# A conditioned decoder trunk in 3-pass fp32r: the first weight slab in plain fp32, first inputs split on two engines, a TensorE run-in, a sixth raw buffer

## The chip, the cores and the metric

The kernel runs on one core of a Trainium2 chip. The metric is the device time of one execution in microseconds (us). Six engines' rows appear in the profile: PE (TensorE matmul), PEld (TensorE weight load), DVE (VectorE), ACT (ScalarE), POOL (GpSimd) and SP (SyncE, which issues the DMAs here).

## The reference

The reference is a decoder trunk of two layers, width 1024, 256 tokens, batch 1. Every sub-layer gets a shift, a scale and a gate from a conditioning vector:

```python
def swiglu(u, w_in, w_out):
    gate, up = jnp.split(u @ w_in, 2, axis=-1)
    return (jax.nn.silu(gate) * up) @ w_out
...
c_act = jax.nn.silu(c)
for l in range(DEPTH):
    mod = c_act @ mod_w[l] + mod_b[l]
    sh1, sc1, g1, ... = jnp.split(mod, 9, axis=-1)
    f = swiglu(x * (1 + sc1) + sh1, ffn_in[l, 0], ffn_out[l, 0])
    x = layer_norm(ALPHA * x + 0.5 * (1 + g1) * f, ...)
    ...   # a mixer (RG-LRU and GLA in layer 0, latent attention in layer 1), then a second swiglu
```

What matters here is the start: the very first matmul needs x * (1 + sc1) + sh1, and sc1 and sh1 need a product of the silu of c with 2 x 1024 x 1024 modulation weights.

## The kernel before, in words

Everything is kept transposed: features on the 128 partitions, the 256 tokens along the free axis. A weight matrix is cut into 128 x 128 tiles, and the host writes the tiles in the exact order of use into `wst`, as slabs of 16 tiles (1 MB). `Stream` (L300) reads this one long list. A slab is loaded into a raw buffer (pool `wraw`, five buffers of 1 MB, L238), and each half of it (8 tiles) is converted by `conv_to` (L329): ScalarE writes the rounded half `whi` (L338), VectorE writes the remainder `wlo` (L339). Three fp32r matmuls then make one product of near-fp32 precision (`mm3`, L403): high weight by high input (L407), high weight by low input (L408), low weight by high input (L409). The inputs are split in the same way by `split` (L443 to L445) into `uhi` and `ulo`.

The modulation weights `modw` use the same raw buffers, in slabs of 1 MB with two 128 x 1024 blocks each. VectorE multiplies a block with the silu of c and sums along the row (`junk`, L388): one block gives one column of a modulation vector. The first eight modulation slabs hold, for each block k of the model width, the shift and the scale of block k.

The first swiglu runs in passes over its 22 pairs of output tiles. The first pass takes 8 pairs (16 PSUM halves) over k = 0 to 3, the second takes 8 other pairs over k = 0 to 7, the third goes back to the first 8 pairs for k = 4 to 7. One k of a pass uses exactly one slab: 16 tiles, 48 matmuls of 256 columns. Step k of the first pass needs, in this order: modulation slab k, the block k of x (`xT`), weight slab k. They are issued in that order on the queue of SP, which runs in order; an issue whose raw buffer is still in use holds all issues behind it. `first_u` (L497) makes input block k: the two `junk` sums, 1 + scale (`scp`, L507, VectorE), the modulated input (`ut`, L509, ScalarE), `uhi` (L444, ScalarE), `ulo` (L445, VectorE) and the scaled residual (`ax`, L511, ScalarE).

The order of instructions on each engine is not written out. A planner sets it at build time, from the order of the program (earlier has priority) and its own idea of when an operand will be there. On the chip each engine then keeps that order, waiting where an operand is late.

Of the kernel before, what the change touches and what calls it, by code (L numbers as in the profile page):

```python
# [11 lines left out]
F32 = mybir.dt.float32  # L12
# [7 lines left out]
MULT, ADD, SUB, MAX, MIN = ALU.mult, ALU.add, ALU.subtract, ALU.max, ALU.min  # L20

P = 128
DM = 1024
KD = DM // P
SEQ = 256
DEPTH = 2
DFF = 2816
NJ = DFF // P
# [22 lines left out]
GLATE = 30  # L51
PAUSE = False
EOFF = 60

FROW = 320
PADS = (128, 64, 416, 352)
# [175 lines left out]
def trunk_kernel(ctx: ExitStack, tc: tile.TileContext, xT, cvec, pos, wst, modw, colsd,  # L232
                 rgw, wa2, outT):
    nc = tc.nc
    sync, act, vec, pool, pe = nc.sync, nc.scalar, nc.vector, nc.gpsimd, nc.tensor

    const = ctx.enter_context(tc.tile_pool(name="const", bufs=1))
    wraw = ctx.enter_context(tc.tile_pool(name="wraw", bufs=5))  # L238
    whi = ctx.enter_context(tc.tile_pool(name="whi", bufs=4))


# [11 lines left out]
    def nm(s):  # L253
        uid[0] += 1
        return f"{s}_{uid[0]}"

    def T(pl, shape, dt=F32, tag=None, **kw):
        return pl.tile(shape, dt, tag=tag, name=nm(tag), **kw)
# [9 lines left out]
    def mmps():  # L268
        return T(ps_mm, [P, 512], tag="mm")
# [19 lines left out]
    ones_dm = constant(1.0 / DM, [P, P], "ones_dm")  # L289
# [6 lines left out]
    ident = T(const, [P, P], tag="ident")  # L296
# [3 lines left out]
    class Stream:  # L300
# [28 lines left out]
        def conv_to(self, n):  # L329

            self.dma_to((n - 1) // 2 + Stream.RAW)
            W2 = Stream.HS * P
            while self.nconv < min(n, 2 * NSLAB):
                s = self.nconv
                hi = T(whi, [P, W2], F32R, tag="whi")
                lo = T(wlo, [P, W2], F32R, tag="wlo")
                raw = self.raw[s // 2][:, (s % 2) * W2:(s % 2 + 1) * W2]
                act.activation(hi, raw, AF.Copy)  # L338
                i = vec.tensor_tensor(lo, raw, hi.bitcast(F32), SUB)  # L339
                if self.behind is not None:  # L340
                    queue_behind(i, self.behind)
                self.conv[s] = (hi, lo)
                if s % 2:
                    self.raw.pop(s // 2)
                self.nconv += 1
                if self.todo and not self.pause and self.todo[0][2] <= s // 2:
                    self.reduce()
                    if len(self.todo) > 4 and self.todo[0][2] <= s // 2:
                        self.reduce()

        def next(self, *keys):
            n = len(keys)
            assert tuple(PLAN[self.pos:self.pos + n]) == keys, (PLAN[self.pos], keys)
            s, o = divmod(self.pos, Stream.HS)
            assert o + n <= Stream.HS
            if o == 0:
                self.conv_to(s + 1 + Stream.AHEAD)
                self.conv.pop(s - 1, None)
            self.pos += n
            hi, lo = self.conv[s]  # L360
            sl = slice(o * P, (o + n) * P)
            return hi[:, sl], lo[:, sl]


        def mod_target(self, s):
# [34 lines left out]
    x0 = T(main, [P, KD, SEQ], tag="yy")  # L400
    W = Stream()

    def mm3(ps, wt, mv, start, stop, shared=False):  # L403

        hi, lo = wt
        mh, ml = mv
        pe.matmul(ps, hi, mh, start=start, stop=False, skip_group_check=shared)  # L407
        pe.matmul(ps, hi, ml, start=False, stop=False, skip_group_check=shared)  # L408
        pe.matmul(ps, lo, mh, start=False, stop=stop, skip_group_check=shared)  # L409

    def queue_behind(i, j):
        tc.add_manual_dep(i.ins, j.ins.name, mybir.DependencyInfo(
            mybir.DependencyClass.NoSync, mybir.DependencyReason.DATA), reason="order")
# [24 lines left out]
    for i in range(2):  # L438
        ps = mmps()
        pe.matmul(ps, one_row, crow[:, i * 512:(i + 1) * 512], start=True, stop=True)  # L440
        ta(cact[:, i * 512:(i + 1) * 512], ps, AF.Silu)

    def split(src, hi, lo):  # L443
        act.activation(hi, src, AF.Copy)  # L444
        vec.tensor_tensor(lo, src, hi.bitcast(F32), SUB)  # L445


    uhi = T(main, [P, KD, SEQ], F32R, tag="uhi")
    ulo = T(main, [P, KD, SEQ], F32R, tag="ulo")
# [6 lines left out]
    def u(k):  # L456
        return uhi[:, k, :], ulo[:, k, :]
# [35 lines left out]
    scp0 = T(const, [P, KD], tag="scp0")  # L493
# [3 lines left out]
    def first_u(k):  # L497
        if k in first_done:
            return
        first_done.add(k)  # L500

        W.mods_to(k + 1)
        while W.todo and W.todo[0][0] < 2 * k + 2:
            W.reduce()
        kk = slice(k, k + 1)
        sc0, sh0 = W.modcols[(0, SC)], W.modcols[(0, SH)]
        vec.tensor_scalar(scp0[:, kk], sc0[:, kk], 1.0, None, ADD)  # L507
        ut = T(wk, [P, SEQ], tag="ut")
        act.activation(ut, x0[:, k, :], AF.Identity, bias=sh0[:, kk], scale=scp0[:, kk])  # L509
        split(ut, uhi[:, k, :], ulo[:, k, :])  # L510
        act.mul(ax[:, k, :], x0[:, k, :], ALPHA)  # L511


    class Boundary:
# [79 lines left out]
        def stats(self, y, ysq):  # L594
# [38 lines left out]
            for m, f in early(*self.next):  # L633
                ps = mmps()
                for k in range(KD):
                    mm3(ps[:, :SEQ + 2], W.next((m, k, f)), [t[:, k, :SEQ + 2] for t in self.ya], k == 0, k == KD - 1)
                with tc.high_priority(offset=EOFF):
                    wab = T(wk, [P, 2], tag="wab", bufs=4)
# [52 lines left out]
    def ffn(l, i, prev):  # L691
        with tc.tile_pool(name=nm("ffn"), bufs=1) as fp:
            hhi = T(fp, [P, NJ, SEQ], F32R, tag="hhi")
            hlo = T(fp, [P, NJ, SEQ], F32R, tag="hlo")
            m = ("ffn_in", l, i)

            def glu(j, pg, pu, bg=0.0, bu=0.0, off=100):
                with tc.high_priority(offset=off):
                    sg = T(wk, [P, SEQ], tag="sg")
                    ta(sg, pg, AF.Silu, bias=bg)  # L700
                    h = T(wk, [P, SEQ], tag="h")
                    vec.scalar_tensor_tensor(h, pu, bu, sg, ADD, MULT)  # L702
                    split(h, hhi[:, j, :], hlo[:, j, :])

            for j in range(EARLY if prev else 0):
                (pg, bg), (pu, bu) = prev.values[2 * j:2 * j + 2]
                glu(j, pg, pu, bg, bu)

            passes = ffn_passes(l, i)
            part = {}  # L710
            for g, ks in passes:
                grp = {j: mmps() if q < 6 else axps() for q, j in enumerate(g)}
                for k in ks:
                    prev.u(k) if prev else first_u(k)
                    for j in g:
                        for half in range(2):
                            mm3(grp[j][:, half * SEQ:(half + 1) * SEQ], W.next((m, k, half * NJ + j)), u(k),
                                k == ks[0] and half == 0, k == ks[-1], True)
                if ks[-1] < KD - 1:
                    keep = [flat(q) for q in range(2)]  # L720
                for q, j in enumerate(g):
                    ps = grp[j]
                    if ks[-1] < KD - 1:
                        part[j] = keep[q // 4][:, (q % 4) * 512:(q % 4 + 1) * 512]
                        act.activation(part[j], ps, AF.Copy)
                        continue
                    off = GOFF
                    if j in part:
                        off -= GLATE * q
                        with tc.high_priority(offset=off):  # L730
                            vec.tensor_tensor(part[j], ps, part[j], ADD)  # L731
                        ps = part[j]
                    glu(j, ps[:, :SEQ], ps[:, SEQ:], off=off)
            if prev:
                prev.residual()
            for j in range(max(g.stop for g, _ in passes), NJ):
                pp = [mmps(), mmps()]
                for half in range(2):
                    for k in range(KD):
                        mm3(pp[half][:, :SEQ], W.next((m, k, half * NJ + j)), u(k),  # L740
                            k == 0, k == KD - 1)
                glu(j, pp[0][:, :SEQ], pp[1][:, :SEQ])
            if l == 0 and i == 0:
                rg_decay()
            if l == 1 and i == 0:
                rope_tables()
            bd = Boundary(l, 0 if i == 0 else 2, 0.5)
            for f in range(KD):
                ps = mmps()
                for k in range(NJ):  # L750
                    mm3(ps[:, :SEQ], W.next((("ffn_out", l, i), k, f)), (hhi[:, k, :], hlo[:, k, :]),
                        k == 0, k == NJ - 1)
                    if f == 1 and k == NJ // 2:
                        bd.shift_out()
                bd.tile_out(f, ps[:, :SEQ])
        return bd
# [559 lines left out]
```

## Time and profile before

| what | us |
|---|---|
| median of 3 runs | 1040.61 |
| lowest and highest of them | 1035.38, 1040.7 |
| the profiled execution, its own time | 1033.83 |
| span of the profiled execution (first to last instruction) | 1032.1 |
| TensorE busy in that span | 995.5 |
| VectorE busy in that span | 884.7 |
| first matmul on a weight slab starts at | 12.03 |

All rows below are from the profiled execution. Its own time lies 1.7 us above its span and 6.8 us below the median of the runs. A row of a timeline gives the start, the busy time, the engine, the line, what is written from what, and in brackets how long the engine had been idle and what released it. TensorE's rows overlap, since matmuls are pipelined: the distance of two starts is the time that one matmul costs.

### The profile page before, as it was taken

The numbers are of one execution on the slowest core, as the hardware profiler recorded it, in microseconds if no ns is written. First come the engines' busy times: TensorE is split into PE (matmuls) and PEld (weight loads), VectorE is DVE, ScalarE is ACT, GpSimd is POOL, SyncE is SP. The second block draws the span as 40 slices with busy tenths as digits, with TensorE's granted clock in tenths as the row PEclk, the third lists the DMA queues.
The fourth block names the chain that finished last, engine by engine and source line by source line (L and its number), as shares of the span: only waits on it lengthen the run. The fifth ranks groups of instructions, "written<-read, shape, count | busy, mean of one in ns | idle before, by whom it ended". The sixth has DMA issues, their size and how long they took to land.

```text
span 1032.1 us, 20703 instructions
## 1 busy us (share of the span) xinstructions
PE 995.5 (96%) x8338; PEld 972.8 (94%) x8338; DVE 884.7 (86%) x1491; ACT 612.5 (59%) x1023; POOL 54.8 (5%) x72
## 2 busy tenths in 40 slices
PE   6999999999999989999999999999999999999995
PEld 5999999998899979999999999999998889999995
DVE  5789999797998989999998899998888799666664
ACT  4746654567886656745545665455559666545543
POOL 0000010000001020000030000002000200000200
PEclk9999999999999999999999999999999999999998
DMA  9998798554466943699977469898743146665621
GB/s 342 366 339 319 257 368 309 208 204 169 170 264 242 350 185 142 245 361 373 365 279 286 166 251 371 322 359 321 286 167 129 73 164 245 246 224 187 243 83 41
DMA packets 38578, 258.57 MB, mean 251 GB/s; under 512 B 4289, under 2 KB 6849, under 8 KB 7762
## 3 DMA queue, kind: packets, MB, share of 16 engines
q1 hardware_dynamic: 38482, 257.25, 66.7%
q8 instruction: 65, 1.06, 0.4%
q14 instruction: 31, 0.25, 0.1%
HBM read 256.18 MB, written 1.05 MB: 249 GB/s over the span
## 4 chain that ended last, share of the span: by engine, by line
PE 82%; DVE 11%; issue 2%; ACT 2%; DMA 2%; POOL 0%; SPq 0%; DVEq 0%; ACTq 0%
PE mm L409 25%; PE mm L407 25%; PE mm L408 25%; DVE wlo L339 4%; DVE junk L388 2%; DMA wraw<-modw 1%; ACT whi L338 1%; DVE flat L557 1%; DVE yy L581 1%; PE ax L408 1%; PE ax L407 1%; PE ax L409 1%; DVE acc L589 1%; DVE flat L731 0%; DMA rgt<-rgw 0%
## 5 line engine op out<-in xcount | busy, mean ns | idle before, releaser
L339 DVE TENSOR_TENSOR wlo<-wraw,whi 128x1024 fp32r<-128x1024 f32 x340 | 416.7, 1233 | 81.3 <-ACT whi L338 80.8
L338 ACT ACTIVATE whi<-wraw 128x1024 fp32r<-128x1024 f32 x340 | 357.6, 1058 | 212.4 <-PE mm L408 138.0
L407 PE MATMUL mm<-uhi,whi 128*128 128x256 f32 x1672 | 461.4, 278 | 11.5 <-ACT uhi L444 6.0
L409 PE MATMUL mm<-uhi,wlo 128*128 128x256 f32 x1672 | 460.1, 277 | 3.6 <-DVE wlo L339 3.6
L408 PE MATMUL mm<-ulo,whi 128*128 128x256 f32 x1672 | 462.1, 277 | 0.7 <-DVE ulo L445 0.6
L407 PEld LDWEIGHTS mm<-uhi,whi 128*128 128x128 f32 x1672 | 313.6, 188 | 14.9 <-ACT uhi L444 7.9
L409 PEld LDWEIGHTS mm<-uhi,wlo 128*128 128x128 f32 x1672 | 313.8, 188 | 4.2 <-DVE wlo L339 4.1
L408 PEld LDWEIGHTS mm<-ulo,whi 128*128 128x128 f32 x1672 | 314.8, 188 | 1.5 <-DVE ulo L445 1.2
L409 PE MATMUL mm<-hhi,wlo 128*128 128x256 f32 x704 | 194.6, 276 | 1.9 <-DVE wlo L339 1.9
L408 PE MATMUL mm<-hlo,whi 128*128 128x256 f32 x704 | 194.4, 276 | 0.0
L407 PE MATMUL mm<-hhi,whi 128*128 128x256 f32 x704 | 194.3, 276 | 0.0
L388 DVE CUSTOM_DVE_ANT_0 junk<-wraw,cact,cols 128x1024 bf16<-128x1024 f32 x144 | 184.9, 1284 | 5.7 <-DMA wraw<-modw 5.0
L409 PEld LDWEIGHTS mm<-hhi,wlo 128*128 128x128 f32 x704 | 132.1, 188 | 2.3 <-DVE wlo L339 2.3
L407 PEld LDWEIGHTS mm<-hhi,whi 128*128 128x128 f32 x704 | 132.2, 188 | 0.0
L408 PEld LDWEIGHTS mm<-hlo,whi 128*128 128x128 f32 x704 | 132.2, 188 | 0.0
L571 POOL TENSOR_TENSOR ax<-ax,shift 128x256 f32<-128x256 f32 x42 | 42.2, 1039 | 734.7 <-ACT shift L569 734.7
L444 ACT ACTIVATE hhi<-h 128x256 fp32r<-128x256 f32 x88 | 35.9, 413 | 44.3 <-DVE h L702 43.2
L585 ACT ACTIVATE ysq<-yy 128x256 f32<-128x256 f32 x42 | 17.4, 414 | 51.8 <-DVE yy L581 50.0
L702 DVE SCALAR_TENSOR_TENSOR h<-mm,sg 128x256 f32<-128x256 f32 x75 | 30.9, 418 | 7.9 <-PE mm L409 7.9
L581 DVE SCALAR_TENSOR_TENSOR yy<-mm,gate,ax 128x256 f32<-128x256 f32 x48 | 22.8, 478 | 16.2 <-PE mm L409 15.0
L445 DVE TENSOR_TENSOR hlo<-h,hhi 128x256 fp32r<-128x256 f32 x88 | 36.0, 417 | 0.0
L429 ACT ACTIVATE sg<-mm 128x256 f32<-128x256 f32 x75 | 27.4, 366 | 3.0 <-DVE h L702 1.7
(288 smaller groups left out, 1088.1 us busy)
## 6 DMA issues: line engine op xcount, KB each, us to landing
wraw<-wst SPq DMA_DIRECT2D x169, 1024.0 KB, 5.8
wraw<-modw SPq DMA_DIRECT2D x71, 1024.0 KB, 6.5
wraw<-modw SPq DMA_DIRECT2D x2, 512.0 KB, 5.4
yy<-xT SPq DMA_DIRECT2D x8, 128.0 KB, 6.8
wraw<-wst SPq DMA_DIRECT2D x2, 512.0 KB, 7.9
rgt<-rgw SPq DMA_DIRECT2D x8, 128.0 KB, 3.7
outT<-yy SPq DMA_DIRECT2D x3, 256.0 KB, 2.6
outT<-yy SPq DMA_DIRECT2D x2, 128.0 KB, 2.6
```

Source lines behind the costliest of these rows:

```text
L338: act.activation(hi, raw, AF.Copy)
L339: i = vec.tensor_tensor(lo, raw, hi.bitcast(F32), SUB)
L388: i = vec.tensor_tensor_reduce(junk, t, cact, 1.0, col("mod_b", (l * NMOD + v) * KD + j), MULT, ADD, self.modcols[(l, v)][:, j:j + 1])
L407: pe.matmul(ps, hi, mh, start=start, stop=False, skip_group_check=shared)
L408: pe.matmul(ps, hi, ml, start=False, stop=False, skip_group_check=shared)
L409: pe.matmul(ps, lo, mh, start=False, stop=stop, skip_group_check=shared)
L429: i = act.activation(out, in_, func, **kw)
L444: act.activation(hi, src, AF.Copy)
L445: vec.tensor_tensor(lo, src, hi.bitcast(F32), SUB)
L571: pool.tensor_tensor(ax[:, j, :], ax[:, j, :], shift, SUB)
L581: vec.scalar_tensor_tensor(y, ps, self.gate[:, f:f + 1], ax[:, f, :], MULT, ADD)
L702: vec.scalar_tensor_tensor(h, pu, bu, sg, ADD, MULT)
```

## The change

Four edits. The first slab (`RAWSLABS = 1`, so k = 0 of the first pass) is not converted: its 16 tiles are multiplied as plain fp32, one matmul each in place of three, with the unsplit `ut` as the input. That input is split after this use (ScalarE and VectorE, L444 and L445), for the second pass. For k from 1 on, `uhi` is computed by VectorE directly from x, while ScalarE computes `ut`; the ScalarE pass `uhi` is gone for these seven blocks. In the program's order, the conversion of the first half of slab 1 and the whole of `first_u(1)` now stand ahead of the matmuls of k = 0. Twelve plain fp32 matmuls of an identity with a constant (128 columns each) are placed behind the two small matmuls that spread c over the partitions; their result is not used. The pool of raw buffers has six buffers.

```diff
-    wraw = ctx.enter_context(tc.tile_pool(name="wraw", bufs=5))
+    wraw = ctx.enter_context(tc.tile_pool(name="wraw", bufs=6))
...
+                if s < 2 * RAWSLABS:
+                    self.conv[s] = (self.raw[s // 2][:, (s % 2) * W2:(s % 2 + 1) * W2], None)
+                    if s % 2:
+                        self.raw.pop(s // 2)
+                    self.nconv += 1
+                    continue
...
+        if lo is None:
+            pe.matmul(ps, hi, mv, start=start, stop=stop, skip_group_check=shared)
+            return
...
+    ps = mmps()
+    for i in range(NWARM):
+        pe.matmul(ps[:, :P], ident, ones_dm, start=True, stop=True)
...
-        split(ut, uhi[:, k, :], ulo[:, k, :])
+        if k < RAWSLABS:
+            u_raw[k] = ut
+        else:
+            vec.tensor_scalar(uhi[:, k, :], x0[:, k, :], scp0[:, kk], sh0[:, kk], MULT, ADD)
+            u_last[0] = vec.tensor_tensor(ulo[:, k, :], ut, uhi[:, k, :].bitcast(F32), SUB)
+            first_ax(k)
...
+                    if not prev and k < RAWSLABS and part == {}:
+                        W.conv_to(2 * RAWSLABS + 1)
+                        first_u(k + 1)
...
+                    if not prev and k in u_raw:
+                        queue_behind(split(u_raw.pop(k), uhi[:, k, :], ulo[:, k, :]), u_last[0])
+                        first_ax(k)
```

## Rows read from the trace of the kernel before

**Rows 1.** The page, busy time, share of the span and instructions by engine.

```profile
PE 995.5 (96%) x8338; PEld 972.8 (94%) x8338; DVE 884.7 (86%) x1491; ACT 612.5 (59%) x1023; POOL 54.8 (5%) x72
```

**Rows 2.** Windows: length, busy us (count) by engine, clock, DMA share, GB/s.

```profile
0.00:12.03 12.03, 3.75 (x4) 1.16 (x4) 3.65 (x13) 5.27 (x10) 1.41 (x14) 1.00 0.78 253
12.03:20.01 7.98, 7.91 (x49) 7.62 (x49) 6.25 (x10) 4.05 (x6) 0.00 (x0) 1.00 1.03 423
20.01:26.46 6.45, 5.60 (x50) 5.40 (x48) 4.74 (x9) 2.54 (x6) 0.00 (x0) 1.00 1.01 414
26.46:33.61 7.15, 5.76 (x49) 5.57 (x49) 5.44 (x9) 3.23 (x6) 0.00 (x0) 1.00 1.01 418
33.61:39.05 5.44, 5.44 (x47) 5.44 (x48) 4.82 (x5) 5.44 (x8) 0.00 (x0) 1.00 0.93 361
```

**Rows 3.** The chain that ended last, 0 to 45 us: start, us, what.

```profile
14.41 1.28 DVE junk L388
15.74 1.28 DVE junk L388
17.07 0.16 DVE scp L507
17.26 0.61 ACT ut L509
17.89 0.42 ACT uhi L444
18.31 0.96 ACT whi L338
19.30 2.36 DVE wlo L339 x2
...
33.61 0.38 PE mm L407
```

**Rows 4.** ACT's timeline, 14 to 62 us.

```profile
14.74 0.42 ACT L511 ACTIVATE ax<-yy 128x256 f32<-128x256 f32 x1 [1.80 <-DMA yy<-xT]
...
18.22 2.00 ACT L338 ACTIVATE whi<-wraw 128x1024 fp32r<-128x1024 f32 x2
...
60.90 0.60 ACT L509 ACTIVATE ut<-yy,mod,scp 128x256 f32<-128x256 f32 x1 [3.62 <-DVE scp L507]
61.41 2.00 ACT L338 ACTIVATE whi<-wraw 128x1024 fp32r<-128x1024 f32 x2
```

**Rows 5.** PE's timeline, 12 to 34 us.

```profile
12.03 1.23 PE L407 MATMUL mm<-uhi,whi 128*128 128x256 f32 x4 [5.96 <-ACT uhi L444]
...
16.05 0.41 PE L407 MATMUL mm<-uhi,whi 128*128 128x256 f32 x1
16.26 0.41 PE L408 MATMUL mm<-ulo,whi 128*128 128x256 f32 x1
...
26.46 0.39 PE L407 MATMUL mm<-uhi,whi 128*128 128x256 f32 x1 [0.85 <-ACT whi L338]
...
33.61 0.38 PE L407 MATMUL mm<-uhi,whi 128*128 128x256 f32 x1 [1.39 <-ACT whi L338]
```

**Rows 6.** PE's timeline at 293 us: plain fp32 matmuls of 256 columns, two rows each.

```profile
293.18 0.59 PE L836 MATMUL ax<-ya,rgt 128*128 128x256 f32 x2
293.61 0.59 PE L835 MATMUL ax<-ya,rgt 128*128 128x256 f32 x2
```

**Rows 7.** Groups by line and shape on DVE: names, shapes, count | busy us, mean ns.

```profile
L673 DVE TENSOR_SCALAR yy<-xh,cols 128x256 f32<-128x256 f32 x2 | 0.8, 413 | 0.1
```

**Rows 8.** PE's timeline, 273 to 279 us.

```profile
273.93 0.38 PE L409 MATMUL mm<-uhi,wlo 128*128 128x256 f32 x1 [1.02 <-DVE wlo L339]
...
278.45 0.38 PE L409 MATMUL mm<-uhi,wlo 128*128 128x256 f32 x1 [1.50 <-DVE wlo L339]
```

**Rows 9.** DVE's timeline at 258 us.

```profile
257.99 1.28 DVE L388 CUSTOM_DVE_ANT_0 junk<-wraw,cact,cols 128x1024 bf16<-128x1024 f32 x1 [0.32 <-DMA wraw<-modw]
```

**Rows 10.** The chain that ended last, 235 to 282 us.

```profile
261.28 4.88 DMA rgt<-rgw
```

More of the change, by code (lines that the diff above doesn't have):

```diff
@@ L53 @@
 EOFF = 60
+RAWSLABS = 1
+NWARM = 12
 FROW = 320
@@ L361, in next @@
             sl = slice(o * P, (o + n) * P)
-            return hi[:, sl], lo[:, sl]
+            return hi[:, sl], None if lo is None else lo[:, sl]
         def mod_target(self, s):
@@ L441, in trunk_kernel @@
         ta(cact[:, i * 512:(i + 1) * 512], ps, AF.Silu)
+    ps = mmps()
+    for i in range(NWARM):
+        pe.matmul(ps[:, :P], ident, ones_dm, start=True, stop=True)
     def split(src, hi, lo):
         act.activation(hi, src, AF.Copy)
-        vec.tensor_tensor(lo, src, hi.bitcast(F32), SUB)
+        return vec.tensor_tensor(lo, src, hi.bitcast(F32), SUB)
     uhi = T(main, [P, KD, SEQ], F32R, tag="uhi")
@@ L509, in first_u, with first_ax @@
         act.activation(ut, x0[:, k, :], AF.Identity, bias=sh0[:, kk], scale=scp0[:, kk])
-        split(ut, uhi[:, k, :], ulo[:, k, :])
+        if k < RAWSLABS:
[4 more added lines that the diff above has]
+            first_ax(k)
+    u_raw = {}
+    u_last = [None]
+    def first_ax(k):
         act.mul(ax[:, k, :], x0[:, k, :], ALPHA)
@@ L714, in ffn @@
                     prev.u(k) if prev else first_u(k)
+                    if not prev and k < RAWSLABS and part == {}:
+                        W.conv_to(2 * RAWSLABS + 1)
+                        first_u(k + 1)
                     for j in g:
                         for half in range(2):
-                            mm3(grp[j][:, half * SEQ:(half + 1) * SEQ], W.next((m, k, half * NJ + j)), u(k),
+                            wt = W.next((m, k, half * NJ + j))
+                            mm3(grp[j][:, half * SEQ:(half + 1) * SEQ], wt, u_raw[k] if wt[1] is None else u(k),
                                 k == ks[0] and half == 0, k == ks[-1], True)
+                    if not prev and k in u_raw:
+                        queue_behind(split(u_raw.pop(k), uhi[:, k, :], ulo[:, k, :]), u_last[0])
+                        first_ax(k)
                 if ks[-1] < KD - 1:
```

## The prediction

> **What bounds the kernel now.** I read the page first, then the windows cut at the starts of the steps k, then the chain of the first 45 us, then the timelines of ScalarE and TensorE inside it. The page makes it a TensorE kernel: 995.5 of 1032.1 us busy [rows 1]. All four edits lie in the first 34 us, where this does not hold. TensorE has no weight to multiply until 12.03 [rows 5], its steps k = 0, 1 and 2 take 7.98, 6.45 and 7.15 us, and only k = 3 runs at its own pace: 48 matmuls in 5.44 us, 0.113 each [rows 2]. Up to 33.61 the chain holds no step that TensorE sets [rows 3]. What repeats in it is a ring between VectorE and ScalarE, once for each k: two sums `junk` (1.28 each, 2.66 from start to start of the next thing), `scp`, `ut`, `uhi`, the first conversion `whi`, two conversions `wlo`, and the sums of the next k. One turn is 7.15 us, the length of the window of k = 2 [rows 2]. TensorE is served by it and waits 0.85 us before k = 2 and 1.39 us before k = 3 [rows 5]. From 33.61 on TensorE sets the end. So the question for each edit is whether it moves the start of k = 3. What moves that start, moves the end by as much, as long as nothing later takes it back.
>
> DMA is the ring's other partner: it is busy without a break from 12 to 34 us at 414 to 423 GB/s [rows 2]. Block 1 of x landed at 14.74 [rows 4]. Modulation slab 1 was issued just ahead of it, so by estimate it landed 0.13 MB / 423 GB/s = 0.31 us earlier, at 14.43, and weight slab 1, issued just behind, lands 1.05 MB / 423 GB/s = 2.48 us later, at 17.2. By the same estimate weight slab 2 lands at 22.5 and slab 3 at 27.8, each with its modulation slab and block of x ahead of it.
>
> **The change, part by part.**
>
> *First slab in plain fp32.* It removes two conversions on ScalarE and two on VectorE (`wlo`, 2.36 for two [rows 3]) and the split of block 0 ahead of the first matmul. So the first matmul can start when `ut` is there. Its place in the ring is `scp` + `ut`, and whether k = 0 is early or late, the sums of k = 1 start when their modulation slab is there: 14.43 by the estimate, against 14.41 in the trace, where they came right behind the second `wlo` [rows 3]. The two conversions had filled a wait for DMA. Gain on the path: 0. On TensorE the slab costs more than before: 16 plain matmuls at 0.43 [rows 6] are 6.9 us, against 48 at 0.113, 5.44. That is 1.4 us of work added beside a ring in which TensorE has idle time, so again 0 on the path. If that cover were gone, it would cost the 1.4.
>
> *Split on two engines.* Here the ring does change. Before, `whi` started 18.22 - 17.26 = 0.96 us after `ut` [rows 3, 4], because `uhi` stood between them on ScalarE; k = 2 and 3 repeat the pattern. After, `whi` follows `ut` directly. The trace has that case at k = 6, where the planner put the conversions first: `whi` starts 61.41 - 60.90 = 0.51 us after `ut` [rows 4]. Saving: 0.45 us a step, and there are three steps (k = 1, 2, 3) between the first sums of k = 1 and the start of k = 3's matmuls: 1.35 us. VectorE takes over seven passes `uhi`. Nearest row: a tensor-scalar of the same shape with two column operands, 0.413 us [rows 7]. It fits while VectorE waits for `ut` and `whi` anyway: `scp` ends at 17.23, `uhi` to 17.65, `ulo` from 17.9 to 18.3, the postponed `ulo` of block 0 to 18.7, and `whi` ends at 17.77 + 1.0 = 18.8. Cost 0. If that cover were gone, each step would pay 0.41 and the gain would be 0.04 a step. I take the cover, since 1.5 us of room stand against 1.3 us of work, and less (0.85) at k = 2 and 3. For k = 4 to 7, four passes of 0.41 fall into a stretch in which TensorE runs without a wait; cost 0.
>
> *Twelve matmuls on a constant.* They start when the matmuls on c end, at 12.03 - 5.96 = 6.07 [rows 5]. A plain matmul of 128 columns is half of 0.43 at full clock and the full 0.43 at half of it: 2.6 to 5.2 us, so TensorE is free again between 8.7 and 11.2. `ut` of k = 0 is ready at about 10.6 by estimate: 12.03 less one `whi` (1.0 [rows 4]) and one `uhi` (0.42 [rows 3]), which followed it. At worst k = 0 starts 0.6 us late; off the path. The clock in the trace: matmuls of 256 columns start 0.21 us apart at 16.05 and 16.26 [rows 5], the lower level, 1.2 GHz, and 0.113 later, the upper level. So it was still low 4.4 us after the first matmul on a slab (16.26 + 0.21 - 12.03), and some 20 matmuls (4.4 / 0.21) cost 0.1 us more each, 2.0 us, all in k = 0. If the run-in raises the clock in the same 4.4 us from 6.07, it is up at 10.5. This shortens k = 0, which isn't on the path: 0. Even if the clock rose only 4.4 us after 11.2, k = 0 would end at 20.3 (5 plain matmuls at 0.86, 11 at 0.43), k = 1 at 25.7, k = 2 at 31.2, before the 32.3 that the ring sets.
>
> *Sixth buffer.* Slab 0 now keeps its buffer until TensorE is through with it, at about 17.7 instead of 14.4. With six buffers the issue of weight slab 2 needs no release and the others move up by one. The DMA engines are busy throughout [rows 2], so earlier issues only lengthen their queue. Cost and gain in the first 34 us: 0. Later the transfers are issued one release earlier everywhere. That can help or hurt in the mixer of layer 0, and stands with the rivals; bounds -2.5 and +2.6.
>
> Sum: 3 x 0.45 = 1.35 us. k = 3 would start at 32.26. The profiled execution would take 1033.83 - 1.35 = 1032.5; the median of the runs lies 6.8 above it, so the forecast is 1040.61 - 1.35 = 1039.3 us. From k = 3 on TensorE has the same work and VectorE practically the same (two `wlo` less, seven `uhi` more, +0.4 us).
>
> **The rivals.**
>
> *The ring opens.* If the planner also lets `whi` run before `ut`, as soon as weight slab k is there (22.5 for k = 2, over an us before that step's `ut`), VectorE's own work sets the pace: two `wlo` 2.36, two sums 2.66, `scp` 0.16, `uhi` and `ulo` about 0.41 each, 6.0 us a step. Then k = 3 starts at 17.07 + 2 x 6.0 + 0.6 = 29.7, 3.9 us earlier: 1036.7. TensorE's own limit lies close by, 10.6 + 6.9 + 2 x 5.44 = 28.4. Against it: in all three steps of the trace the order was `ut` first, although the conversion stands earlier in the program, so the planner expected the slab after `ut`, and nothing in the change makes slabs arrive earlier. The Trainium skill, page "Perfetto Trace Analysis", section Identifying the Most-Contended Engine, says to take the engine with the highest occupancy, for TensorE by its weight loads, and to improve that one first. By that rule TensorE (weight loads 94%) is the bound, the plain slab alone would lengthen the kernel by its 1.4 us to 1042.0, and an earlier, faster start would give its time back in full, about this rival's 1036.7. The chain of the first 34 us, in which TensorE sets no step, speaks against it.
>
> *The sixth buffer pays in the mixer.* At 257.99 VectorE had been waiting for a modulation slab [rows 9]; its two sums (2.66) then ran ahead of everything else, and TensorE waited for `wlo` at 273.93 and 278.45, 2.5 us together [rows 8]. With a slab issued one release earlier the sums could run earlier too, and the 2.5 are gone: 1036.8 with the sum above. Against it: VectorE keeps its order, and in that order the slab was late by only 0.3 us [rows 9].
>
> *Slower: the small loads queue behind one more slab.* In the same place the gate weights `rgt` share SP's queue with the slabs; their transfer is on the chain with 4.88 us [rows 10]. One more slab issued ahead of them adds 1.05 MB at 414 GB/s, 2.5 to 2.6 us, which TensorE then waits for at 278. It decides as soon as the slab stands ahead of `rgt` on the queue, since `wlo` is late there already [rows 8]. 1040.61 - 1.35 + 2.6 = 1041.9, or 1043.2 if the ring gains nothing either.
>
> *It doesn't do what it says.* VectorE's order may put `uhi` or the late split where they hold the `wlo`; then the 0.45 is lost: 1040.6.
>
> **How the numbers follow.** Forecast 1039.3: 0.57. Ring opens 1036.7: 0.15. Mixer gains 1036.8: 0.11. Slower 1041.9: 0.10. No effect 1040.6: 0.07. Range: down to 1034.0, about the opened ring and the mixer's 2.5 together (1036.7 - 2.5 = 1034.2), and the lowest run shown less the sum (1035.38 - 1.35); up to 1043.2. A difference of 0.5% (5.2 us) is about what a measurement of this kernel can tell from no change: its runs shown span 5.3 us. Faster by more than that takes two gains at once, or a run of luck in the medians: 0.20. Slower by more takes the queue twice or an order that I don't see: 0.07. Within: 0.73.
>
> **What would show it.** Right: `whi` about 0.5 us behind `ut` for k = 1 to 3, `scp` 6.7 us apart, k = 3's first matmul at 32 to 32.6 with a wait for `whi` before it, k = 0 done well before k = 1 starts, no wait longer than before at 274 to 279. Wrong: k = 3 at 29 to 30 with `whi` ahead of `ut`; `wlo` late behind `uhi`; TensorE waiting nowhere between k = 0 and k = 3, which would mean that it paces the start; or a different set of waits after 100 us, by which the planner's new order decides more than the start does.

## The result and the profile after

The changed kernel is slower, not faster. Its 22 runs have a median of 1040.19 us (1036.35 to 1043.63), the 22 runs of the kernel before beside them 1036.81 us (1033.26 to 1042.25). The ratio is 1.0033 with a 95% interval of 1.0018 to 1.0047, which is +3.4 us, between 1.9 and 4.9. The three runs of before on which the forecast stood had drawn a median 3.8 us above the one that 22 runs give, so the forecast's 1039.3 lies near 1040.19 by that alone, which is luck; its step, -1.35, had the wrong sign.

The profiled execution of after took 1039.56 us with a span of 1037.8, 5.7 us longer than before's span. The start did what it was to do. The windows of after, cut at the starts of the run-in, of the plain slab (k = 0) and of k = 1, 2 and 3 (columns as in [rows 2]):

```profile
6.10:11.30 5.20, 5.20 (x25) 5.20 (x26) 3.19 (x11) 2.13 (x5) 0.00 (x0) 1.00 1.02 385
11.30:18.20 6.90, 6.90 (x34) 6.05 (x33) 4.46 (x9) 2.55 (x4) 0.00 (x0) 1.00 1.01 417
18.20:24.43 6.23, 5.80 (x51) 5.58 (x49) 5.32 (x10) 2.38 (x5) 0.00 (x0) 1.00 1.02 416
24.43:31.18 6.75, 5.76 (x48) 5.57 (x48) 5.84 (x10) 2.89 (x5) 0.00 (x0) 1.00 1.02 423
```

The clock column reads 1.00 in the first of these windows, and in 12.03:20.01 of [rows 2], but the starts of the matmuls tell otherwise there: those of the run-in lie 0.43 us apart for 128 columns, and in before those of the first slab 0.21 apart for 256 until 16.5 [rows 5], both the lower level.

k = 3 starts at 31.18 in place of 33.61, 2.43 us earlier. The chain of after shows the shorter ring; beside [rows 3], `uhi` is gone from it:

```profile
4.03 9.17 DMA wraw<-modw
13.22 1.28 DVE junk L398
14.55 1.28 DVE junk L398
15.88 0.16 DVE scp L525
16.06 0.60 ACT ut L527
16.66 0.96 ACT whi L348
17.64 2.36 DVE wlo L349 x2
20.00 1.20 DVE junk L398
...
31.18 0.38 PE mm L420
```

Its first sum starts at 13.22, 1.19 earlier than before's, and the path from there to k = 3 takes 17.96 in place of 19.20.

The loss lies behind 150 us. TensorE's waits of after between 120 and 200 us, and then between 255 and 330 us (us in total, times, longest); before had 2.9 and 2.5 us there, all for `wlo`, and one of 1.06 at 349.79 that after does not have:

```profile
PE mm L422 <- DVE wlo L349: 4.6, 3, 1.8
```

```profile
PE mm L422 <- DVE wlo L349: 4.1, 2, 3.7
PE ax L870 <- DMA rgt<-rgw: 1.3, 2, 1.0
```

The wait of 3.70 is new; it answers to the 1.50 of [rows 8]. SP's timeline, first of before and then of after, shows how it comes about:

```profile
253.10 0.33 SPq L372 DMA_DIRECT2D wraw<-modw  x1
256.41 1.19 SPq L829 DMA_DIRECT2D rgt<-rgw  x2
257.70 0.38 SPq L325 DMA_DIRECT2D wraw<-wst  x1
```

```profile
253.86 0.33 SPq L328 DMA_DIRECT2D wraw<-wst  x1
256.40 0.33 SPq L382 DMA_DIRECT2D wraw<-modw  x1
257.19 1.19 SPq L864 DMA_DIRECT2D rgt<-rgw  x2
```

One slab of weights and one modulation slab that stood behind the second pair of `rgt` now stand ahead of it, and the pair takes 4.4 us to land where it took 1.9. The chain of after goes on from there:

```profile
257.19 4.41 DMA rgt<-rgw
...
271.05 1.15 DVE ya L885
272.27 3.72 POOL ya L886
...
279.49 1.15 DVE wlo L349
280.68 0.39 PE mm L422
```

On VectorE the four scans of the RG-LRU wait 2.30 us for GpSimd, and the `wlo` that TensorE needs is queued behind them. In before the scans stand ahead of that `wlo` too, but wait for nothing. VectorE's timeline, before and then after:

```profile
270.56 3.31 DVE L339 TENSOR_TENSOR wlo<-wraw,whi 128x1024 fp32r<-128x1024 f32 x1
273.80 2.43 DVE L853 TENSOR_TENSOR_SCAN flat<-ya,ya 128x256 f32<-128x256 f32 x4
...
277.18 1.21 DVE L339 TENSOR_TENSOR wlo<-wraw,whi 128x1024 fp32r<-128x1024 f32 x1
```

```profile
272.50 1.22 DVE L349 TENSOR_TENSOR wlo<-wraw,whi 128x1024 fp32r<-128x1024 f32 x1
276.01 2.44 DVE L888 TENSOR_TENSOR_SCAN flat<-ya,ya 128x256 f32<-128x256 f32 x4 [2.30 <-POOL ya L886]
...
279.41 1.22 DVE L349 TENSOR_TENSOR wlo<-wraw,whi 128x1024 fp32r<-128x1024 f32 x1
```

The rest of the loss is the clock. In three stretches of 3.4 us the granted clock of after fell to the lower level, 1.2 GHz: from 233.5, 281.3 and 390.5. Before's profile has none there. Windows of after around the second and the third:

```profile
277.00:280.70 3.70, 0.02 (x1) 0.03 (x1) 3.70 (x8) 2.15 (x6) 0.00 (x0) 1.00 0.20 82
280.70:284.70 4.00, 4.00 (x21) 4.00 (x22) 4.00 (x8) 2.21 (x4) 0.00 (x0) 0.58 0.28 90
386.00:390.50 4.50, 2.60 (x23) 2.40 (x23) 4.50 (x11) 3.32 (x6) 0.43 (x1) 1.00 0.46 189
390.50:394.00 3.50, 3.50 (x19) 3.50 (x18) 2.93 (x5) 0.51 (x2) 0.00 (x0) 0.51 0.00 0
```

Matmuls of 256 columns start 0.21 apart in such a stretch in place of 0.113. Some 16 of them at 0.1 more each make about 1.5 us a drop: between two ends of `yy` on VectorE just before and just behind the third one (390.09 and 395.37), the lag on before grows from 4.07 to 5.62. The account of the profiled span is then: start -2.4; waits between 120 and 200 +1.7; waits between 255 and 360 +1.8 (5.4 against 3.6); three drops +4.6; sum +5.7.

Before's profile has no drop in the middle of the kernel. Its mean clock, 0.996, is that of 34 of the 121 runs of before in the experiments below, and of none of after's 22. Over the runs the mean granted clock was 0.9909 for after (22 runs) and 0.9940 to 0.9946 for before (four sets of 23 to 35 runs). One drop takes half the clock for 3.4 of 1036 us, 0.00165 of the mean; so by estimate after had about two drops more per run, some 3.1 us, nearly the size of the whole loss. The start's gain and the new waits leave about +1 in the profile; the two together, 4.2, are more than the 3.4 measured, but inside its interval. Three runs of those below took over 200 us longer than the others (2594.13 of before, 1254.46 of after with five buffers, 1440.89 of late scans without the run-in) and are left out of every ratio and mean.

### The profile page after: what moved, and what is told of

It reads as the page before. It is cut to its first block, busy times and chain, and to the rows that moved or that the text cites. A ratio compares the mean times of both kernels' runs of the same rounds, so it can differ in the third digit from the quotient of the medians.

```text
span 1037.8 us, 20733 instructions
## 1 busy us (share of the span) xinstructions
PE 1004.5 (97%) x8346; PEld 981.7 (95%) x8346; DVE 885.2 (85%) x1496; ACT 607.7 (59%) x1014; POOL 58.0 (6%) x72
## 3 DMA queue, kind: packets, MB, share of 16 engines
q8 instruction: 65, 1.06, 0.4%
## 4 chain that ended last, share of the span: by engine, by line
PE 85%; DVE 9%; DMA 2%; issue 1%; ACT 1%; POOL 1%; SPq 0%; DVEq 0%; ACTq 0%
PE mm L420 25%; PE mm L421 25%; PE mm L422 25%; DVE wlo L349 2%; DVE junk L398 2%; DMA rgt<-rgw 1%; DMA wraw<-modw 1%; PE mm L1020 1%; PE mm L1021 1%; PE mm L1022 1%; PE ax L420 1%; PE ax L421 1%; PE ax L422 1%; DVE yy L609 0%; DVE acc L617 0%
## 5 line engine op out<-in xcount | busy, mean ns | idle before, releaser
L349 DVE TENSOR_TENSOR wlo<-wraw,whi 128x1024 fp32r<-128x1024 f32 x338 | 411.0, 1224 | 80.6 <-ACT whi L348 80.1
L609 DVE SCALAR_TENSOR_TENSOR yy<-mm,gate,ax 128x256 f32<-128x256 f32 x48 | 22.9, 478 | 17.7 <-PE mm L422 16.5
L420 PE MATMUL mm<-flat,whi 128*128 128x258 f32 x96 | 28.7, 298 | 0.0
```

Of the source, the lines that this page charges most:

```text
L609: vec.scalar_tensor_tensor(y, ps, self.gate[:, f:f + 1], ax[:, f, :], MULT, ADD)
```

## The experiments

Theories named in the expectations: A, the sixth buffer changes the order of later work; B, the edits of the start change it; C, the loss is drops of the clock, whatever the waits; others where they come up. All ratios are to the kernel before, run beside each version on the same chip; the versions ran on four chips, and those of different chips are compared only through before. The clock is the mean granted clock over the runs of the version; waits of TensorE and the last column, in us, are those of its profile.

| version | ratio, 95% interval | mean clock | waits 120-200 | waits 255-330 | first sum of k = 1 to k = 3 |
|---|---|---|---|---|---|
| before | 1 | 0.994 | 2.9 | 2.5 | 19.20 |
| after | 1.0033 [1.0018, 1.0047] | 0.9909 | 4.6 | 5.4 | 17.96 |
| before, six buffers | 1.0032 [1.0020, 1.0044] | 0.9916 | 4.2 | 4.9 | 19.19 |
| after, five buffers | 0.9995 [0.9978, 1.0012] | 0.9940 | 3.2 | 2.4 | 17.97 |
| after, no run-in | 1.0020 [1.0007, 1.0033] | 0.9919 | 4.5 | 4.8 | 17.97 |
| before, split on two engines | 0.9986 [0.9971, 1.0000] | 0.9941 | 2.9 | 2.4 | 17.97 |
| after, slab 0 of its own, ring of five | 0.9999 [0.9983, 1.0016] | 0.9938 | 2.7 | 2.5 | 17.96 |
| after, four `rgt` buffers | 1.0008 [0.9990, 1.0027] | 0.9926 | 4.6 | 3.9 | 17.97 |
| slab 0 of its own, four `rgt` | 1.0010 [0.9992, 1.0028] | 0.9924 | 4.3 | 2.4 | 17.97 |
| before, four `rgt` | 0.9985 [0.9969, 1.0002] | 0.9948 | 2.9 | 2.4 | 19.20 |
| after, late scans | 0.9978 [0.9964, 0.9991] | 0.9946 | 4.6 | 2.2 | 17.97 |
| after, late scans, four `rgt` | 0.9987 [0.9974, 1.0000] | 0.9942 | 4.6 | 2.1 | 17.97 |
| before, split, four `rgt` | 1.0007 [0.9994, 1.0021] | 0.9923 | 4.2 | 2.4 | 17.97 |
| after, wait filled | 1.0041 [1.0028, 1.0053] | 0.9925 | 4.6 | 3.1 | 17.97 |
| before, late scans | 1.0001 [0.9986, 1.0015] | 0.9942 | 3.1 | 2.1 | 19.20 |
| after, late scans, no run-in | 0.9978 [0.9964, 0.9992] | 0.9947 | 4.6 | 2.2 | 17.98 |

**The sixth buffer alone**, in the kernel before:

```diff
-    wraw = ctx.enter_context(tc.tile_pool(name="wraw", bufs=5))
+    wraw = ctx.enter_context(tc.tile_pool(name="wraw", bufs=6))
```

> The kernel before with one edit, the sixth raw buffer. Theory A (the sixth buffer moves later work: the loads of `rgt` go onto SP's queue behind more slabs, and sums `junk` get ahead of `wlo` on VectorE): k = 3 starts at 33.6 us as before, but TensorE waits about 3 us in all near 157 to 162 and over 3 us between 261 and 304, so the span is 4 to 8 us longer than before's 1032.1, and the median ratio is 1.004 to 1.008. Theory B (the edits of the start, not the buffer, upset the later plan): waits and span as before, ratio 1.000. Theory C (the changed kernel's extra time is all drops of the granted clock): ratio 1.000 plus or minus what such drops give, waits as before.

Measured: 1.0032, the whole loss, with the start of before. Its waits between 255 and 330 us:

```profile
PE mm L409 <- DVE wlo L339: 4.6, 2, 3.7
PE ax L835 <- DMA rgt<-rgw: 0.3, 1, 0.3
```

So B falls: none of the edits of the start is needed for the loss. The profiled span is 6.8 us longer than before's, inside A's 4 to 8, with three drops of the clock in it; over all runs the ratio is a little under A's 1.004.

**The changed kernel with five buffers** (the same line the other way round).

> The changed kernel with five raw buffers, so all edits of the start without the sixth buffer. Theory A: k = 3 starts about 2 us earlier than before (31.2 to 32.3 us), the waits behind 100 us are those of before, so the span is 1029.5 to 1031 and the median ratio 0.9975 to 0.999. Theory B: the waits near 157 to 162 and 261 to 304 are those of the changed kernel, ratio 1.003. Theory C: waits as before, but drops of the granted clock after 200 us, ratio above 1.001.

Measured: 0.9995, k = 3 at 32.56, the long wait gone. The start gains less here than in after, since its first sum of k = 1 came at 14.59, and one drop fell at 165.9. A holds for the waits; k = 3, the span (1033.9) and the ratio all came out above its ranges. The gain of the start is inside the noise of this measurement.

**No run-in** (`NWARM = 0` in the changed kernel).

> The changed kernel without the twelve matmuls on a constant. Theory A (and my step that the run-in lies off the path): k = 0 runs at the lower clock for longer, k = 3 starts within 0.3 us of the changed kernel's 31.18, waits after it are the same, median ratio to before 1.003 as for the changed kernel. Theory C (the run-in brings the clock's drops later on): ratio 1.000 or less. If the run-in carries the start, k = 3 starts 1 to 2 us later and the ratio is 1.004 to 1.005.

Measured: 1.0020, k = 3 at 31.95, outside the 0.3 us that I had allowed. Its later start is that of its first sum, 13.97 against 13.22; from there it takes 17.97 as all others with the split do. The run-in is off the path, and it does not bring the loss.

**The split on two engines alone**, in the kernel before, for all eight steps:

```diff
-        split(ut, uhi[:, k, :], ulo[:, k, :])
+        vec.tensor_scalar(uhi[:, k, :], x0[:, k, :], scp0[:, kk], sh0[:, kk], MULT, ADD)
+        vec.tensor_tensor(ulo[:, k, :], ut, uhi[:, k, :].bitcast(F32), SUB)
```

> The kernel before with one edit, the split of the first inputs on two engines (`uhi` on VectorE from x, `ulo` from `ut`) for all eight steps, five buffers, no plain slab, no run-in. By my sum three turns of 0.45 us: k = 3 starts at 32.3 us, the rest as before, median ratio 0.9987. If most of the 2.4 us that the changed kernel gains at k = 3 hangs on the plain slab (modulation slab 1 lands earlier or its sums start earlier), the gain here is 1.0 to 1.4 us and no more; if the split alone opens the ring it is 2 us or more.

Measured: k = 3 at 32.29, 1.32 earlier than before, of which 1.23 are the shorter path and 0.09 an earlier first sum. The ratio is 0.9986, -1.4 us, but its interval reaches 1 and the plain medians, 1035.76 and 1036.11, lie less than 0.4 us apart: that the whole gain arrives at the end is not shown. Its chain runs as in the changed kernel, with `whi` straight behind `ut`:

```profile
16.98 0.16 DVE scp L507
17.16 0.60 ACT ut L509
17.76 0.96 ACT whi L338
18.75 2.36 DVE wlo L339 x2
21.11 1.20 DVE junk L388
```

**Slab 0 in a buffer of its own**, the ring at five: the space of six buffers, with every engine's order that of the five-buffer version.

```diff
-    wraw = ctx.enter_context(tc.tile_pool(name="wraw", bufs=6))
+    wraw = ctx.enter_context(tc.tile_pool(name="wraw", bufs=5))
+    wraw0 = ctx.enter_context(tc.tile_pool(name="wraw0", bufs=1))
-                t = T(wraw, [P, SLAB * P], tag="wraw")
+                t = T(wraw if s else wraw0, [P, SLAB * P], tag="wraw")
```

> The changed kernel with slab 0 in a buffer of its own and the ring at five: the same space as with six raw buffers and no release for slab 1 to 5 to wait on at the start, but every engine's order of instructions is that of the five-buffer version of the changed kernel. Theory A (the order that goes with a ring of six costs the time): the waits of `before` behind 100 us (`rgt` issued near 111 us, no wait for `rgt` at 262, `wlo` waits of 0.9 and 1.5 near 275 and 280 in place of 3.70), k = 3 between 31.2 and 32.6, median ratio 0.997 to 0.9995. Theory D (the space itself, other addresses for everything that is allocated behind the raw buffers, or the earlier transfers cost it): the waits of the changed kernel, ratio 1.002 to 1.004.

Measured: 0.9999, a little above A's range, waits as in before. Its one row between 255 and 330 us:

```profile
PE mm L423 <- DVE wlo L350: 2.5, 2, 1.5
```

So it is not the space or the addresses; the loss goes with the ring of six. The traces show what the ring changes: VectorE, ScalarE and GpSimd do their work in the same order here as in the five-buffer version; SP's queue has one order in all five versions with a ring of five and two buffers for `rgt`, and another in all six with a ring of six. Whether it is this order or the earlier releases, late scans tell, further down: they keep the ring of six and change the order.

**Four buffers for `rgt`** in the changed kernel (`bufs=4` on the tile `rgt`, L863).

> The changed kernel with four buffers in place of two for the gate weights `rgt`; ring of six. Theory A1 (the late second pair of `rgt`, which now stands behind a slab and a modulation slab on SP's queue, makes the 3.70 us wait): all four loads are issued together near 187 us, TensorE's wait of 0.30 at 262 is gone, the 3.70 near 281 shrinks to 0 to 1.5, and the waits of 1.61 and 1.80 near 157 to 162 stay; span 2 to 4 us below the changed kernel's 1037.8, median ratio 0.9995 to 1.0015. Theory A2 (the order on VectorE alone, the scan ahead of `wlo`, makes it): a wait of over 3 us for `wlo` stays near 281, ratio 1.002 to 1.004.

Measured: between the two theories. No wait for `rgt` is left, but a wait of 3.65 for `wlo` is:

```profile
PE mm L422 <- DVE wlo L349: 3.9, 2, 3.6
```

GpSimd's `ya` now ends earlier and the scans wait for nothing, but they still run ahead of `wlo`, and TensorE, which no longer waits for `rgt` and had no drop near 233 in this profile, reaches the place earlier: the wait ends at 276.65 against 280.68. The ratio, 1.0008, is 2.6 us better than the changed kernel's: 1.5 us of waits, and by the mean clock one drop fewer. By these figures the late `rgt` pair is about half of the loss, but the two intervals overlap.

**Both of these together**, and **four `rgt` buffers in the kernel before**.

> The changed kernel with slab 0 in a buffer of its own, the ring at five, and four buffers for `rgt`: the version that theory A would build. If the 4.88 us of the `rgt` transfer on the chain of before set the waits of 1.02 and 1.50 for `wlo` near 275 and 280, they go, and the span is 2 to 4 us below before's 1032.1, median ratio 0.995 to 0.998. If those two waits are set by the sums `junk` of the modulation slab, they stay, and the ratio is that of the version with slab 0 of its own, 0.997 to 0.9995.

> The kernel before with four buffers for `rgt` and nothing else. If `rgt` sets the waits for `wlo` near 274 and 278, the span is 1 to 2.5 us shorter than before's 1032.1, median ratio 0.9975 to 0.999; if the sums of the modulation slab set them, 1.000 within 0.001, with start and other waits as before.

Measured: 0.9985 for before with four buffers, where the waits of 0.9 and 1.5 stay and a third, the 1.06 that before has at 349.79, is gone; the interval holds 1. The expectation had named the wrong wait. With slab 0 of its own the same edit gives 1.0010, above both ranges of the expectation: the waits of 0.9 and 1.5 stay there too, and a wait of 3.09 at 165.7 stands in the place of 1.56 and 0.13.

**Late scans.** The changed kernel with the first four scans behind the queries in the program; on VectorE they then stand behind the `wlo`.

```diff
-                for q in range(RB):
-                    vec.tensor_tensor_scan(xa[:, j0 + q, :SEQ], ww[:, q, :], tz[:, q, :], 0.0, MULT, ADD)
+                def scans():
+                    for q in range(RB):
+                        vec.tensor_tensor_scan(xa[:, j0 + q, :SEQ], ww[:, q, :], tz[:, q, :], 0.0, MULT, ADD)
+                return scans
...
-                elif step == "q": queries()
+                elif step == "q":
+                    queries()
+                    scans()
...
-                    rglru(4 * "RS".index(step))
+                    scans = rglru(4 * "RS".index(step))
+                    if step == "S":
+                        scans()
```

> The changed kernel with one edit: the four scans of the first half of the RG-LRU stand behind the queries in the program, so that VectorE takes `wlo` first and no longer waits 2.30 us for GpSimd's `ya` with `wlo` queued behind it. Theory A2 (that order makes the wait of 3.70): it shrinks to under 1.5 us, the waits of 1.61 and 1.80 near 160 and the 0.30 for `rgt` near 262 stay; span 2 to 4 us below the changed kernel's 1037.8, median ratio 1.000 to 1.002. Theory C2 (the drops of the granted clock follow from long waits of TensorE): the drop near 281 goes with the wait, and the mean granted clock of the runs rises by about 0.0015 from the changed kernel's 0.991. If the drops have to do with something else, the mean clock stays 0.991 and the gain is under 2.5 us.

Measured: 0.9978, 5.7 us better than the changed kernel (each against before beside it) and, with the version below that has no run-in, the lowest ratio of all. VectorE's timeline and TensorE's waits between 255 and 330 us:

```profile
275.08 1.21 DVE L349 TENSOR_TENSOR wlo<-wraw,whi 128x1024 fp32r<-128x1024 f32 x1
...
282.53 2.42 DVE L889 TENSOR_TENSOR_SCAN flat<-ya,ya 128x256 f32<-128x256 f32 x4
```

```profile
PE mm L422 <- DVE wlo L349: 0.8, 2, 0.6
PE ax L988 <- DVE scores L980: 0.5, 1, 0.5
PE ax L870 <- DMA rgt<-rgw: 0.5, 1, 0.5
PE ax L978 <- DVE la L1011: 0.4, 1, 0.4
```

Theory A2 holds: with the ring of six and its order on SP's queue kept, an edit of VectorE's order takes the long wait away. The gain is larger than either theory said: 3.2 us of waits, and the mean clock rose by 0.0037, two drops, where I had counted on the one near 281.

> The changed kernel with the scans late and four buffers for `rgt`, so both causes of the 3.7 us wait removed in the ring of six. Theory A: TensorE's waits between 255 and 330 sum to under 2 us (before: 2.5, changed kernel: 5.5), the waits near 160 stay at 3.4, the span in an undisturbed run is 1029 to 1031, median ratio 0.998 to 1.0. If the ratio stays at the 1.0008 that four buffers for `rgt` alone gave, the order on VectorE is not what is left.

Measured: 0.9987. The waits between 255 and 330 sum to 2.1, as with late scans alone, but nearly all of it is one wait of 1.88 for `wlo` at 274.23, with a drop right behind it. Four `rgt` buffers add nothing that these runs can tell once the scans are late.

**The two edits that had gained alone**, split and four `rgt` buffers, in the kernel before.

> The kernel before, ring of five, with the split on two engines and four buffers for `rgt`: the two edits that gained alone (0.9986 and 0.9985). If they add, as two mechanisms in two places should: k = 3 at 32.0 to 32.4, no wait near 350, median ratio 0.997 to 0.9975. If one of the two was luck or the planner's order takes it back, 0.9985 to 1.0005.

Measured: 1.0007; they do not add. The order at 160 us changed once more, with three sums `junk` between two `wlo` where before has two, and the granted clock was at the lower level from 165.0 to 171.8. TensorE's waits from 150 to 180 us:

```profile
PE mm L409 <- DVE wlo L339: 3.1, 1, 3.1
```

**The wait filled.** The changed kernel with 14 matmuls on a constant in the first query, between its second matmul and the third:

```diff
+                    if f == 16 and k == 0:
+                        (hi, lo), (mh, ml), pd = W.next((m, k, f)), u(k), mmps()
+                        pe.matmul(ps[:, :SEQ], hi, mh, start=True, stop=False)
+                        pe.matmul(ps[:, :SEQ], hi, ml, start=False, stop=False)
+                        for _ in range(14):
+                            pe.matmul(pd[:, :P], ident, ones_dm, start=True, stop=True)
+                        pe.matmul(ps[:, :SEQ], lo, mh, start=False, stop=False)
+                        continue
```

> The changed kernel with 14 matmuls on a constant placed in the wait of 3.70 us near 281, between the second matmul of the first query and the third, which waits for `wlo`; about 14 x 0.22 = 3.1 us of TensorE work that nobody reads. Theory C2 (an idle TensorE brings the clock's drop): no drop within 5 us behind that place, mean granted clock of the runs 0.9925 against 0.991, ratio 1.000 to 1.002. If the drop comes all the same, the idle time is not what brings it: mean clock 0.991, ratio 1.003 or more.

Measured: 1.0041, as the second branch has it, and a mean clock of 0.9925, as the first has it. At the place itself 0.69 us of wait is left, and no drop came within 5 us; but the planner wrote another order behind it, with a new wait of 1.31 at 288.44 and a drop at 289.2. It doesn't settle what sets a drop off.

**Late scans in the kernel before, and late scans without the run-in.**

> The kernel before, ring of five, with the late scans and nothing else. Theory A (the ring of six made the scan's place harmful; with five the waits of 1.02 and 1.50 near 274 and 278 have another cause): median ratio 0.999 to 1.001, the two waits stay, so what the changed kernel with late scans gains over before, 0.9978, is the start's. Theory E (late scans are a gain by themselves, in either ring): the two waits go, the span is 1.5 to 2.5 us below before's 1032.1, ratio 0.9975 to 0.9985, and of the changed kernel's edits none is needed for most of the gain.

> The changed kernel with the late scans and without the twelve matmuls on a constant. If the run-in is off the path, the ratio is that of the version with it, 0.9978 within 0.001, and k = 3 starts at 18.0 us behind the landing of modulation slab 1, as in the other versions with the split. If it carries part of the gain, k = 3 starts 0.5 us or more later than that and the ratio is 0.9985 to 1.000.

Measured: 1.0001 and 0.9978. In the ring of five late scans are worth nothing that the runs show: of the two waits one stays (1.07 at 274.16), and 0.44 and 0.63 for other work stand in the place of the second. So what they give in the ring of six takes back what that ring did. Without the run-in the version is as fast as with it.

That the 0.9978 is the gain of the start alone, as theory A has it, is not shown. The profiled span of the version with late scans is 2.0 us below before's: k = 3 is 2.19 earlier, the waits between 120 and 200 us take 1.7 back, and those between 255 and 360 are 1.4 shorter than before's. And the two versions with the whole start in a ring of five, 0.9995 and 0.9999, show no clear gain.

## Why the prediction was wrong

*What bounds the start: right.* VectorE and ScalarE set it. TensorE waits 0.43 us before k = 2 and 0.99 before k = 3, where [rows 5] have 0.85 and 1.39.

*Split on two engines, 1.35: right, 10% too large.* From the first sum of k = 1 to k = 3 takes 19.19 to 19.20 us in the four profiles without it and 17.96 to 17.98 in the twelve with it: 1.23 us, to within 0.02. VectorE's passes `uhi` had the cover that I gave them, at least those of k = 1 to 3, which lie on this path.

*The ring opens: no.* `whi` stayed behind `ut` in all three steps, and a turn, from first sum to first sum, took 6.7 to 6.8 us, not 6.0. By the rule set beside that rival (the Trainium skill, page "Perfetto Trace Analysis", section Identifying the Most-Contended Engine), TensorE would have been the engine to improve; in this stage an edit that takes nothing off TensorE, the split alone, shortened the path to its k = 3 by 1.23 us, so the trace speaks against the rule here.

*First slab in plain fp32, 0: roughly right.* The 16 matmuls took the 6.9 us that I summed, off the path. The first sum of k = 1 starts right behind the landing of its modulation slab, at 13.22 to 14.59 us over the ten profiles with the plain slab. Over the six without it starts at 13.96 to 14.41, and in three of them the second `wlo` of block 0 ends within 0.05 us of that start (14.40 in before, where the slab landed at 14.38); with six buffers in the kernel before, the slab had landed at 13.96 and the `wlo` held the sum until 14.33. So the conversions that I took for a filler end level with the landing, and without the plain slab a landing as early as after's could not have been used in full. In after the slab landed early, which is the other 1.19 of the 2.43; means of 13.86 and 14.30 make it about 0.4. What moves the landing from run to run stays open.

*Twelve matmuls on a constant, 0: right.* k = 0 followed them at 11.28, at the late end of my range (11.2), and leaving them out changed nothing clear of the noise in either version. Their starts lie 0.43 apart to the last, so the clock was still at the lower level then, and my "up at 10.5" was early; the slab's matmuls, 16 in 6.9 us, ran at the upper level.

*Sixth buffer, 0 in the first 34 us, -2.5 to +2.6 later: here it failed.* The start was as said. Later, I costed it as one release earlier in the order of before and put the chance of harm at 0.10. In fact the planner wrote another order for a ring of six, and that edit alone gave 1.0032, the whole loss; I had named another order only as one of the things that would prove me wrong. The rival "the small loads queue behind one more slab" had the right place and the right first step: the slab stands ahead of the second pair of `rgt`, and TensorE starts on that pair at 261.73, 3.1 us later than in before (TensorE's timeline of before, 254 to 262 us):

```profile
258.60 0.59 PE L835 MATMUL ax<-ya,rgt 128*128 128x256 f32 x2
```

It missed what hangs on that load: GpSimd's `ya`, the scans, and the `wlo` queued behind them. The sentence that VectorE keeps its order, by which I argued against the mixer's gain, was the same mistake.

*The size of a lost wait.* I priced a wait at its length. The 3.2 us of waits that late scans remove were worth 5.7, with two drops fewer per run beside them; that the waits bring the drops is likely from the counts below, but not shown.

*The base.* A median of three runs, and a profile free of drops, were both taken for the kernel's own time. They stand 3.8 us above and 3 us below the median of 22.

What stays open: what exactly sets off a drop; and why the planner puts more sums ahead of `wlo` near 160 us in the ring of six, which still costs 1.7 us of waits in the version with the lowest ratio. A version that takes it back wasn't tried.

## What to carry to other kernels

A buffer count is an input of the planner, not only a release: before costing another buffer at nothing, compare the order of the queues and of the bounding engine's feeder at the far end of the kernel, above all where a small load shares a queue with the slabs. When a local gain is lost far away, undo the parts one at a time: the one-line part that I had costed at nothing carried the whole loss here, and the cure was to move four instructions behind the one that TensorE waits for. And take the base from many runs, and ask whether the profile of before has a typical clock.

## What the hardware showed that I had not expected

The granted clock falls to the lower level for 3.4 us in the middle of the kernel, most often behind a wait of TensorE, and not every time. In the 16 profiles, behind 100 us, a drop began in or within 2 us behind 5 of the 6 waits of over 3 us, 8 of the 26 between 1.7 and 2.0, and 2 of the 102 between 0.8 and 1.7. The same wait for `yy` had none in before, where it ended at 386.07 after 1.92 us, and one in after, where matmuls then start 0.21 apart:

```profile
390.15 0.39 PE L420 MATMUL mm<-uhi,whi 128*128 128x256 f32 x1 [1.90 <-DVE yy L609]
...
391.94 0.41 PE L420 MATMUL mm<-uhi,whi 128*128 128x256 f32 x1
392.15 0.41 PE L421 MATMUL mm<-ulo,whi 128*128 128x256 f32 x1
```

Seven drops had no such wait ahead: five between 232 and 237, next to groups of four matmuls that use 16 of the 128 rows, and two at 839 to 841, within 1.3 us of a wait of 0.71. A drop or two more or less is a good part of the 9 us over which the runs of one kernel scatter.

VectorE and GpSimd hold each other up. While GpSimd multiplied `ya` in before, a `wlo` of VectorE took 3.31 us in place of 1.22; in after, where the `wlo` beside it kept its 1.22, `ya` took 3.71 in place of 2.40 (GpSimd's spans are rough). GpSimd's timeline, before and then after:

```profile
270.39 2.40 POOL L851 TENSOR_TENSOR ya<-ya 128x1024 f32<-128x1024 f32 x1 [61.11 <-DVE ya L850]
```

```profile
272.27 3.71 POOL L886 TENSOR_TENSOR ya<-ya 128x1024 f32<-128x1024 f32 x1 [63.80 <-DVE ya L885]
```

In both cases one of the two takes as long as both after each other: 3.31 against 1.22 + 2.40 = 3.62, and 3.71. The Trainium skill, page "SBUF — State Buffer", section SBUF: two separate sides, has the rule for it: a VectorE instruction with two inputs in SBUF and a GpSimd instruction that reads SBUF need the same pair of ports, the first of them holds the pair for its whole instruction, and the other is fully blocked. The rows agree that one waits for the other; which of them came first they don't show, since GpSimd's starts are rough. Nor is every instruction of VectorE held: in the trace of late scans, beside `ya` from 271.16 to 274.87, `bc` and `lb`, which take one input from a matmul's result, kept their 0.41, while `xh` took 1.97 in place of 0.48.
